# Row sums of a 32 x 512 x 1024 array: each 16-row load issued as two 8-row halves from two engines

## The chip, the cores and the metric

The kernel runs on one core of a Trainium2 chip. The metric is the device time of one execution in microseconds (us). Before the change it is 161.86 us, the median of three runs (161.58 to 162.03).

## The reference

```python
def setup_inputs():
    batch, seq, dim = 32, 512, 1024
    return {"x": np.random.randn(batch, seq, dim).astype(np.float32)}

def reference(x):
    return np.sum(x, axis=-1).astype(np.float32)
```

There are 16,384 rows of 1,024 float32 values, 67.1 MB to be read, and one sum per row to be written, 65.5 KB.

## The kernel before

The rows are cut into 8 groups of 2,048. In a group, each of the 128 partitions holds 16 consecutive rows (`BIG = 16`), which are 64 KB that lie together in HBM. A load of a whole group fills a tile of 128 x 16,384 float32. The tiles come from a pool with three buffers, so a fourth tile has to wait until the first has been read.

The order of the work is written out by hand, with no scheduler. The last group is treated in pieces, so that the kernel starts and ends with something small:

1. The first load (`FIRST = 7`) brings rows 0 to 6 per partition of the last group. It is moved to the program's entry, ahead of the barrier at which the engines meet. VectorE sums its seven rows with one `tensor_reduce` (line 141).
2. Then come the seven other groups, g = 0 to 6, one load of 16 rows each (line 180). Groups 0 to 5 are summed by VectorE, one `tensor_reduce` of 128 x 16,384 each. Of group 6, VectorE sums nine rows one by one with a custom instruction that adds the two halves of a row and accumulates (`halves`, line 155), and ScalarE sums seven with an activation that accumulates (`act`, line 168).
3. At the end come the rest of the last group: a load of six rows, one of two rows, and the last row in two pieces of 560 and 464 values (lines 222 and 223). VectorE and ScalarE share the six and the two rows; VectorE sums the two pieces.
4. Two stores write the sums: ScalarE issues that of the first seven groups (line 191, from line 224), SyncE that of the last group.

All loads are issued by SyncE, in this order. An instruction that issues a DMA waits on its engine's queue, in order, for what it needs: the load of group 1 is held until the seven-row reduction is done (`hold`, line 208), the load of group 2 takes the first buffer again, and each later load waits for the reduction that last read its buffer, that of group 3 for group 0's and so on. The last group's remaining loads use the buffer of group 4.

The functions that the change touches are `rows` (line 177), which issues a load and the sums of its rows, and the loop over the groups that calls it (lines 201 to 208).

Of the kernel before, what the change touches and what calls it, by code (L numbers as in the profile page):

```python
# [100 lines left out]
@with_exitstack  # L101
def kernel(
    ctx: ExitStack,
    tc: tile.TileContext,
    x: bass.AP,
    out: bass.AP,
):
    nc = tc.nc
    nc.at_finalize(issue_first_load_at_entry)
    nc.at_finalize(order_waits)  # L110
    nc.at_finalize(wait_for_the_store_at_the_clear)
    fp32 = mybir.dt.float32
    P = 128
    batch, seq, dim = x.shape
    rows = batch * seq
    J = rows // P
    BIG = 16


    x_g = x.flatten_outer_dims().rearrange("(g p j) d -> g p j d", p=P, j=BIG)  # L120
    out_v = out.rearrange("b s -> (b s)").rearrange("(g p j) -> p g j", p=P, j=BIG)

    def rows_from(j, n):
        return x_g[j // BIG, :, j % BIG : j % BIG + n, :]

    last = J // BIG - 1
    FIRST = 7
    pieces = (560, 464)  # L130

    with (
        tc.tile_pool(name="in", bufs=3) as inpool,
        tc.tile_pool(name="unread", bufs=4, space=bass.MemoryType.PSUM) as upool,
        tc.tile_pool(name="stage", bufs=1) as stpool,
        tc.manual_schedule(),
    ):
        sums = stpool.tile([P, J], fp32)

        def vec(dst, src):  # L140
            return nc.vector.tensor_reduce(  # L141
                out=dst, in_=src, axis=mybir.AxisListType.X, op=mybir.AluOpType.add
            )

        def hold(inst, until, reason):
            tc.add_manual_dep(
                inst.ins,
                until.ins.name,
                mybir.DependencyInfo(mybir.DependencyClass.Sync, mybir.DependencyReason.DATA),
                reason=reason,  # L150
            )

        def halves(dst, src):
            n = src.shape[-1] // 2
            return nc.vector.tensor_tensor_reduce(  # L155
                out=src[:, :n],
                in0=src[:, :n],
                in1=src[:, n:],
                scale=1.0,
                scalar=0.0,  # L160
                op0=mybir.AluOpType.add,
                op1=mybir.AluOpType.add,
                accum_out=dst,
            )

        def act(dst, src, n):
            unread = upool.tile([P, dim], fp32)
            nc.scalar.activation(  # L168
                out=unread[:, :n],
                in_=src,  # L170
                func=mybir.ActivationFunctionType.Copy,
                accum_out=dst,
            )

        sums_of = []

        def rows(t, a, n, j, n_act, pairs=False):
            nv = n - n_act
            block = t[:, a * dim : (a + n) * dim].rearrange("p (n d) -> p n d", d=dim)
            load = nc.sync.dma_start(out=block, in_=rows_from(j, n))  # L180
            if pairs:
                for q in range(nv):
                    sums_of.append(halves(sums[:, j + q : j + q + 1], block[:, q, :]))
            else:
                sums_of.append(vec(sums[:, j : j + nv], block[:, :nv, :]))
            for q in range(nv, n):
                act(sums[:, j + q : j + q + 1], block[:, q, :], dim)
            return load

        def store(eng, g0, g1):  # L190
            return eng.dma_start(
                out=out_v[:, g0:g1],
                in_=sums[:, g0 * BIG : g1 * BIG].rearrange("p (g j) -> p g j", j=BIG),
            )


        j = last * BIG
        t = inpool.tile([P, BIG * dim + 4], fp32)
        rows(t, 0, FIRST, j, 0)
        first = sums_of[-1]  # L200
        for g in range(last):
            t = inpool.tile([P, BIG * dim + 4], fp32)
            if g < last - 1:
                load = rows(t, 0, BIG, g * BIG, 0)
            else:
                rows(t, 0, BIG, g * BIG, 7, pairs=True)
            if g == 1:
                hold(load, first, "no descriptors of later loads while the first ones start")

        t = inpool.tile([P, BIG * dim + 4], fp32)  # L210
        rows(t, FIRST, 6, j + FIRST, 2, pairs=True)
        two = rows(t, FIRST + 6, 2, j + FIRST + 6, 1, pairs=True)
        a = BIG - 1

        j += a
        c, width = pieces
        whole = t[:, a * dim + c : BIG * dim + 2]
        nc.vector.memset(whole[:, width + 1 :], 0.0)  # L220
        part = t[:, a * dim : a * dim + c]
        nc.sync.dma_start(out=part, in_=rows_from(j, 1)[:, 0, :c])  # L222
        nc.sync.dma_start(out=whole[:, 1 : width + 1], in_=rows_from(j, 1)[:, 0, c:])
        hold(store(nc.scalar, 0, last), two, "its packets come behind those of the loads")
        halves(whole[:, :1], part)
        halves(sums[:, j : j + 1], whole)
        store(nc.sync, last, last + 1)
# [30 lines left out]
```

## Time and profile before

| what | value |
|---|---|
| time, median of three runs | 161.86 us (161.58 to 162.03) |
| span of the profiled execution | 159.9 us, no other time is given for that execution |
| VectorE (DVE) busy | 120.6 us, 75% |
| ScalarE (ACT) busy | 12.0 us, 8% |
| read from HBM | 67.11 MB, 420 GB/s over the span |
| a 16-row load, from issue to landing | 40.8 us, median of seven |

A span runs from the first to the last instruction; the time of an execution includes what lies around it. "From issue to landing" includes the time that a load stands behind other loads. A queue (q1, q10) is what one engine issues: q1 is SyncE's and q10 is ScalarE's. The transfers themselves run on 16 DMA engines that the core has. A DMA is cut into packets; here a packet of a load is one partition's share, so that each of the 16 engines moves 8 packets of a load over 128 partitions. In the profile DVE is VectorE, ACT is ScalarE, SP is SyncE, and SPq or ACTq is such an engine's issue of a DMA.

### The profile page before, as it was taken

What the parts mean: (1) busy time and instruction counts of PE and PEld (TensorE: products, weight loads), DVE (VectorE), ACT (ScalarE), POOL (GpSimd) and SP (SyncE); (2) the same over time, 40 slices, a digit from 0 to 9 for tenths busy, and PEclk for the clock granted to TensorE, in tenths of its full rate; (3) what the DMA queues carried; (4) which work ended last, traced back from release to release, by engine and by line L of the source; (5) the groups of instructions that cost most, each with busy time, mean ns of one, the idle gap of its engine ahead of it and who ended that gap; (6) DMA issues with size and microseconds to landing.
All of it is one profiled execution on the core that took longest, in us unless ns stands there. A gap on an engine that the chain in (4) does not pass through costs nothing.

```text
span 159.9 us, 132 instructions
## 1 busy us (share of the span) xinstructions
DVE 120.6 (75%) x40; ACT 12.0 (8%) x21; POOL 0.2 (0%) x4
## 2 busy tenths in 40 slices
DVE  0029600499985999779995899949999499994955
ACT  3000000000000000000000000000000000003993
POOL 0000000000000000000000000000000000000000
DMA  8899899799699699699699699799898996996994
GB/s 308 380 492 525 361 426 525 328 459 525 295 492 525 262 525 525 262 525 525 262 525 508 279 525 476 312 525 410 377 525 361 426 525 262 525 525 289 400 384 124
DMA packets 2784, 67.18 MB, mean 420 GB/s; under 512 B 1248, under 2 KB 1376, under 8 KB 1504
## 3 DMA queue, kind: packets, MB, share of 16 engines
q1 hardware_dynamic: 1872, 67.12, 97.7%
q10 hardware_dynamic: 912, 0.06, 0.4%
HBM read 67.11 MB, written 0.07 MB: 420 GB/s over the span
## 4 chain that ended last, share of the span: by engine, by line
DMA 71%; DVE 27%; SPq 1%; issue 0%; DVEq 0%
DMA t<-in_x_dram 71%; DVE sums L141 26%; SPq L180 0%; SPq L222 0%; DVE t L155 0%; DVEq L253 0%
## 5 line engine op out<-in xcount | busy, mean ns | idle before, releaser
L141 DVE TENSOR_REDUCE sums<-t 128x16 f32<-128x16384 f32 (+1 forms) x7 | 110.9, 15848 | 33.4 <-DMA t<-in_x_dram 33.4
L168 ACT ACTIVATE unread<-t 128x1024 f32<-128x1024 f32 x10 | 10.1, 1013 | 144.7 <-DMA t<-in_x_dram 144.7
L155 DVE CUSTOM_DVE_ANT_0 t<-t 128x512 f32<-128x512 f32 (+2 forms) x16 | 9.6, 654 | 4.1 <-DMA t<-in_x_dram 4.0
L168 ACT ACTIVATION_READ_ACCUMULATOR unread<-t 128x1 f32 x10 | 1.9, 188 | 0.0
L168 ACT ACT_TABLE_LOAD x1 | 1.3, 1283 | 0.8 <-PEq L242 0.8
L155 DVE DVE_READ_ACCUMULATOR2_ANT sums<- 128x1 f32 x15 | 1.2, 81 | 0.0
L242 POOL MEMSET const-bfloat16-1.0<- 128x1 bf16 x1 | 0.1, 102 | 0.0
L242 POOL MEMSET const-uint8-127<- 128x1 uint8 x1 | 0.1, 102 | 0.0
L242 POOL MEMSET const-float32-1.0<- 128x1 f32 x1 | 0.1, 99 | 0.0
L242 POOL MEMSET const-float32-0.0<- 128x1 f32 x1 | 0.1, 98 | 0.2 <-issue 0.2
L155 DVE DVE_READ_ACCUMULATOR2_ANT t<- 128x1 f32 x1 | 0.1, 83 | 0.0
L220 DVE MEMSET t<- 128x1 f32 x1 | 0.1, 59 | 0.0
## 6 DMA issues: line engine op xcount, KB each, us to landing
t<-in_x_dram SPq DMA_DIRECT2D x1, 3584.0 KB, 11.0
t<-in_x_dram SPq DMA_DIRECT2D x1, 3072.0 KB, 28.9
t<-in_x_dram SPq DMA_DIRECT2D x1, 1024.0 KB, 31.0
t<-in_x_dram SPq DMA_DIRECT2D x1, 280.0 KB, 31.2
t<-in_x_dram SPq DMA_DIRECT2D x1, 232.0 KB, 31.3
t<-in_x_dram SPq DMA_DIRECT2D x7, 40.8
out_dram<-sums ACTq DMA_DIRECT2D x1, 56.0 KB, 2.1
out_dram<-sums SPq DMA_DIRECT2D x1, 8.0 KB, 1.4
```

The costliest lines, as they stand in the source:

```text
L141: return nc.vector.tensor_reduce(out=dst, in_=src, axis=mybir.AxisListType.X, op=mybir.AluOpType.add)
L155: return nc.vector.tensor_tensor_reduce(out=src[:, :n], in0=src[:, :n], in1=src[:, n:], scale=1.0, scalar=0.0, op0=mybir.AluOpType.add, op ...
L168: nc.scalar.activation(out=unread[:, :n], in_=src, func=mybir.ActivationFunctionType.Copy, accum_out=dst,)
L220: nc.vector.memset(whole[:, width + 1 :], 0.0)
L242: nc = _bacc.Bacc("TRN2", target_bir_lowering=False, num_devices=1)
```

## The change

A load of 16 rows per partition is issued as two loads of 8 rows, the first half by SyncE and the second by ScalarE, both into the same tile. The other loads (seven, six, two rows and the two pieces) stay as they are. The hold on group 1's load is put on both halves.

```diff
         def rows(t, a, n, j, n_act, pairs=False):
             nv = n - n_act
             block = t[:, a * dim : (a + n) * dim].rearrange("p (n d) -> p n d", d=dim)
-            load = nc.sync.dma_start(out=block, in_=rows_from(j, n))
+            if n == BIG:
+                h = n // 2
+                load = [
+                    nc.sync.dma_start(out=block[:, :h, :], in_=rows_from(j, h)),
+                    nc.scalar.dma_start(out=block[:, h:, :], in_=rows_from(j + h, h)),
+                ]
+            else:
+                load = nc.sync.dma_start(out=block, in_=rows_from(j, n))
...
             if g == 1:
-                hold(load, first, "no descriptors of later loads while the first ones start")
+                for half in load:
+                    hold(half, first, "no descriptors of later loads while the first ones start")
```

In the compiled program ScalarE's queue begins with seven loads of 128 x 8,192, ahead of its table load and its activations. Each `tensor_reduce` waits for both halves of its load. In group 6, VectorE's first eight rows wait for SyncE's half alone; its ninth row and ScalarE's seven rows wait for ScalarE's half.

## The prediction

> **What bounds the kernel now.** I read the engine shares and the DMA queues on the page first.
>
> ```profile
> span 159.9 us, 132 instructions
> ...
> DVE 120.6 (75%) x40; ACT 12.0 (8%) x21; POOL 0.2 (0%) x4
> ...
> q1 hardware_dynamic: 1872, 67.12, 97.7%
> q10 hardware_dynamic: 912, 0.06, 0.4%
> ```
>
> q1 holds everything that SyncE issues, q10 what ScalarE issues. The 16 DMA engines are at work for 97.7% of the span on q1, VectorE for 75%. The chain of waits says the same from the end:
>
> ```profile
> 0.00 11.01 DMA t<-in_x_dram
> ...
> 126.33 31.29 DMA t<-in_x_dram
> 157.62 0.07 issue
> 157.69 0.40 DVE t L155
> ```
>
> The last load lands at 157.62 and one 0.40 us reduction and the store follow. The timeline shows what lies between (start, length, engine; in brackets the idle time before it and who ended it):
>
> ```profile
> 11.03 7.62 DVE L141 TENSOR_REDUCE sums<-t 128x7 f32<-128x7168 f32 x1 [11.03 <-DMA t<-in_x_dram]
> 30.34 17.22 DVE L141 TENSOR_REDUCE sums<-t 128x16 f32<-128x16384 f32 x1 [11.69 <-DMA t<-in_x_dram]
> 49.69 17.22 DVE L141 TENSOR_REDUCE sums<-t 128x16 f32<-128x16384 f32 x1 [2.14 <-DMA t<-in_x_dram]
> ...
> 127.09 17.22 DVE L141 TENSOR_REDUCE sums<-t 128x16 f32<-128x16384 f32 x1 [2.13 <-DMA t<-in_x_dram]
> ...
> 146.50 0.69 DVE L155 CUSTOM_DVE_ANT_0 t<-t 128x512 f32<-128x512 f32 x1 [2.19 <-DMA t<-in_x_dram]
> ...
> 153.87 0.69 DVE L155 CUSTOM_DVE_ANT_0 t<-t 128x512 f32<-128x512 f32 x1 [1.78 <-DMA t<-in_x_dram]
> ```
>
> VectorE waits about 2.1 us for each 16-row load, and they land 19.35 us apart: 8.39 MB each, 433.5 GB/s. The trace's packet records (start and length of every packet) show why. Each of the 16 engines moves 8 packets of 65,536 B per load, 2.418 us long, and the next starts 2.414 us after the one before. The engines are back to back until the last load; no gap in the middle is there to be won. Only less work or a faster packet could shorten the path.
>
> The span is 2.0 us below the median, 161.86. The page gives no other time for the profiled execution, so I carry those 2.0 us over unchanged.
>
> **Part 1: more packets.** A load's 8 packets per engine of 65,536 B become 16 of 32,768 B. The spacing of packets in the records is 2.414 us at 65,536 B, 1.058 us at 28,672 B and 0.908 us at 24,576 B: a line with 0.0368 ns per byte and 3.3 ns per packet. A 32,768 B packet then takes 1.209 us. Seven loads with 8 more packets each cost 56 x 3.3 ns = 0.18 us. Each load ends with a 4-byte packet per engine that counts it done; the next data packet starts 6 ns later. Seven more of these: 0.04 us. All of it is on the path: **+0.22 us**.
>
> That 6 ns row also stands against a rule: the Trainium skill, DMA: Bandwidth & Descriptors, section "Anatomy of one DMA — SWDGE (gpsimd) path", fits about 2.0 us fixed per DMA for those that GpSimd issues. By it, seven more DMAs paid one after the other would cost 14 us. Here the queue's next load starts behind the count packet, so the trace does not charge this.
>
> **Part 2: turns between two rings.** SyncE's and ScalarE's packets now meet on the same engines. The trace of before never shows that: ScalarE's only transfer begins after the loads' last packet. The cost of a turn is bounded below by a gain, the 3.3 ns of each packet hidden behind the other ring (-0.2 us at most for 56 added packets), and above by the longest stretch that a packet in mid-stream shows: some 24,576 B packets near 149 us take about 1.03 us for 0.912, 0.12 us more. With 16 packets per load and engine, at most 112 turns in all, that far end is +13 us. Nearest is the 6 ns row, which is one load giving way to the next on an engine; it is counted already. I take zero for the turn itself.
>
> **Part 3: the issues.** ScalarE issues seven loads ahead of its table load. Before, its queue looked like this:
>
> ```profile
> 0.78 1.28 ACT L168 ACT_TABLE_LOAD   x1 [0.78 <-PEq L242]
> ...
> 146.50 1.03 ACT L168 ACTIVATE unread<-t 128x1024 f32<-128x1024 f32 x1 [144.44 <-DMA t<-in_x_dram]
> ```
>
> The compiled order puts the table load behind the seventh issue, which waits for the reduction of the fourth 16-row load (88.40 + 17.22 = 105.6 us, about 108 below). Its 1.28 us is over by 110, and the first activation is due at 146: 36 us of cover; without it, 1.28 us would come ahead of the ten activations. SyncE's issue count is unchanged (0.33 to 0.44 us each, hidden).
>
> **Part 4: the first load gets company.** ScalarE's first half-load waits for nothing. It leaves at about 0.78 us, where the table load stood, and its packets come some 1.0 us later (the first load's packet starts at 1.02 us, that of ScalarE's store 0.95 us after its issue), so at about 1.8 us, during the first load's first packet. With turns in equal measure, 7 of its packets go between the first load's 8: landing at 11.01 + 7 x 1.21 = 19.5 instead of 11.0, the seven-row reduction ends at 27.1 instead of 18.65, and the hold on the second 16-row load is released then, for both issuers. Packets follow at 28.1. The engines have work until 30.0 (30.34 less 0.36 from last packet to VectorE's start), as the bytes up to there are the same. The cover shrinks from 10.3 us (30.0 - 18.7 - 1.0) to 1.9. Were all 8 packets served first, it would be 20.7, 28.3, 29.3: 0.7 us of cover. So no gap: nothing on the path.
>
> **Part 5: a load is done when its later half is.** At 28.1 SyncE's ring still has (30.0 - 28.1) / 1.21 = 1.6 packets of the first 16-row load, ScalarE's none: up to two packets of the next load slip in, and that load completes up to 2 x 1.21 = **2.4 us later**, at 32.8. ScalarE's ring stays two packets ahead, so each following load completes 2.4 us later too. Only in the last one does it run dry, and SyncE's half finishes where all bytes finish: 146.5 + 0.2. What is late is VectorE: its last long reduction ends at 144.31 + 2.4 + 0.2 = 146.9 instead of 144.31, its nine row sums take 5.6 us (146.50 to 152.10) and end at 152.5. The six-row load lands at 153.87 + 0.2. Its cover was 2.19 + 1.78 = **3.97 us**, 1.5 stay. If it is used up, the excess goes to the end almost one for one, as VectorE's idle time after 153.87 is under 0.2 us. Late buffers hurt nothing: group 3's load is issued at 50.0 while the rings hold work until 69; the tail's loads at 127.6, with work until 146.5.
>
> The sum: 0.22 + 0 = +0.2 us, span 160.1, time **162.1 us**. A measurement can tell about 0.3%, 0.49 us, from no change: this forecast lies within.
>
> A page states the sharing itself: the Trainium skill, DMA: Bandwidth & Descriptors, section "Queues, rings and completion order", has each engine go round the rings packet by packet. No run here shows it; by it part 4 holds as written, with strict order by ring it would be the third rival. The forecast needs less: any lead of one half up to 3.97 us gives the same time.
>
> **Rivals.**
> 1. *VectorE comes late.* If ScalarE's packets begin two to four rounds later (at 3.7 to 6 us, a slow first issue), four of them precede the first load's end, it lands at 15.9, the release is early (24.5 with packets), and the lead is four packets, 4.8 us. That is 0.9 over the cover: 162.1 + 0.9 = 163.0. For it: nothing shows ScalarE's first issue. Against: the table load was up at 0.78.
> 2. *Turns cost* — the rival that is surely slower. At each of about 112 turns an engine loses what its smallest packet takes in all, 7 to 12 ns (64 B, 4 B rows): +0.8 to +1.3 us, 162.9 to 163.4. It decides from 2.4 ns a turn (0.27 us more). At the far end of part 2, 175. For it: alternate packets read other rows of HBM. Against: between different DMAs 6 ns suffice.
> 3. *One ring is served first*, SyncE's say. Then ScalarE's half of the first 16-row load waits for three of SyncE's, lands near 49.7, and VectorE runs back to back: six reductions (103.3 us) to 153, nine rows to 158.6, and what took from 153.87 to 158.09 to 162.8: +4.7, 166.6 us. For it: no row. Against: nothing gives one issuer precedence.
> 4. *Faster.* The first load's first packets take 1.3 to 1.9 us instead of 1.06; ScalarE's could fill up to 0.7 us of that, 161.4. Against: the excess may be HBM's, and more packets are then slow as well.
> 5. *It does not split anything in time*: the halves follow each other. Time as forecast; the compiled order shows the seven issues on ScalarE, so I fold this in.
>
> **Numbers.** Forecast 0.56; VectorE late 0.14 (0.08 of it beyond 0.3%); turns cost 0.16, far end 0.04; one ring first 0.04; faster 0.06. Slower: 0.08 + 0.16 + 0.04 + 0.04 = 0.32. Same: 0.56 + 0.06 = 0.62. Faster 0.06. The range, 161.6 to 163.6, takes in the forecast with the 0.2 us spread of the runs, rival 1 and the near end of rival 2; about 0.18 stays out.
>
> **What would show it.** Part 1: packets of about 1.209 us when alone, q1 and q10 at half each of most bytes, share of both together near 98%. Part 4: the seven-row reduction starts near 19.5. Part 5: 16-row reductions start about 2.4 later than before but 19.4 apart, VectorE's wait ahead of the row sums is gone, the activations start near 144 since ScalarE's half lands early. Rival 2: landings more than 19.5 apart. Rival 1: no wait before the six-row load's sums. I am wrong if the landings drift apart, or if an engine stands empty near 30 us.

## The result and the profile after

The changed kernel takes **162.71 us** (median of four runs, 162.70 to 162.75) against 161.84 us; the ratio is 1.0064 with a 95% interval of 1.0052 to 1.0076. That is slower by some 0.9 us, beyond the 0.3% that a measurement can tell from no change. The forecast was 162.1 us, too near the old time to be told from it. The time lies in the stated range (161.6 to 163.6), but the likeliest case did not come, and the step that failed has to be found.

The engine shares and queues of the changed kernel's page (busy time, share of the span, number of instructions; then each queue's packets, MB and share of the 16 engines' time):

```profile
span 160.6 us, 149 instructions
...
DVE 120.6 (75%) x40; ACT 11.9 (7%) x21; POOL 0.2 (0%) x4
...
q1 hardware_dynamic: 1872, 37.76, 55.2%
q10 hardware_dynamic: 1920, 29.42, 42.9%
```

Both queues together fill 98.1% of the span, as before (97.7 and 0.4): the engines move the same bytes in more time. VectorE's work is the same to 0.1 us. The two issuers, ScalarE's table load and the long waits of VectorE in the changed kernel's timeline:

```profile
0.76 105.99 ACTq L184 DMA_DIRECT2D t<-in_x_dram  x7
0.77 105.95 SPq L183 DMA_DIRECT2D t<-in_x_dram  x7
18.46 7.62 DVE L141 TENSOR_REDUCE sums<-t 128x7 f32<-128x7168 f32 x1 [18.46 <-DMA t<-in_x_dram]
30.70 17.22 DVE L141 TENSOR_REDUCE sums<-t 128x16 f32<-128x16384 f32 x1 [4.61 <-DMA t<-in_x_dram]
50.22 17.22 DVE L141 TENSOR_REDUCE sums<-t 128x16 f32<-128x16384 f32 x1 [2.30 <-DMA t<-in_x_dram]
...
106.79 1.28 ACT L168 ACT_TABLE_LOAD   x1 [106.79 <-DVE sums L141]
...
127.93 17.22 DVE L141 TENSOR_REDUCE sums<-t 128x16 f32<-128x16384 f32 x1 [2.22 <-DMA t<-in_x_dram]
...
147.18 0.69 DVE L155 CUSTOM_DVE_ANT_0 t<-t 128x512 f32<-128x512 f32 x1 [2.03 <-DMA t<-in_x_dram]
147.35 1.03 ACT L168 ACTIVATE unread<-t 128x1024 f32<-128x1024 f32 x1 [39.28 <-DMA t<-in_x_dram]
...
154.50 0.69 DVE L155 CUSTOM_DVE_ANT_0 t<-t 128x512 f32<-128x512 f32 x1 [1.72 <-DMA t<-in_x_dram]
```

The first reduction starts at 18.46 instead of 11.03, so the first load did share its engines. But group 0's starts at 30.70, only 0.36 late, not 2.4. Then the lateness grows slowly: 0.53 at 50.22, 0.84 at 127.93, 0.63 at 154.50. From group 1 on VectorE still waits about 2 us for each load; it is never the one that is late. The end of the chain of waits:

```profile
126.59 31.15 DMA t<-in_x_dram
157.74 0.02 issue
157.77 0.47 DVE t L155 x2
...
158.37 0.40 DVE t L155
```

The end is set by loads as before, 0.68 us later (158.37 against 157.69).

A second thing is not in these rows. The time of a run less its span was 2.15 to 2.21 us in the four runs of the changed kernel (spans are given to 0.1 us). In the 62 runs of the kernel before that stood beside the experiments, it was 1.73 to 1.83, and the mean 1.79. So **about 0.4 of the 0.9 us lies outside the span**, where the prediction had carried 2.0 us over unchanged. (These 2.0 were the median of some runs less the span of one profiled execution.)

The theory after this look (A): the cost has nothing to do with two rings; it is the price of more packets, and something outside the span. The rival (B): packets cost what was predicted, and the second ring the rest.

### The profile page after: what moved, and what is told of

The parts are those of the page before. It is cut to its first block, busy times and chain, and to the rows that moved or that the text cites. A ratio compares the mean times of both kernels' runs of the same rounds, so it can differ in the third digit from the quotient of the medians.

```text
span 160.6 us, 149 instructions
## 1 busy us (share of the span) xinstructions
DVE 120.6 (75%) x40; ACT 11.9 (7%) x21; POOL 0.2 (0%) x4
## 4 chain that ended last, share of the span: by engine, by line
DMA 71%; DVE 27%; SPq 0%; issue 0%; DVEq 0%
DMA t<-in_x_dram 71%; DVE sums L141 26%; DVE t L155 1%; SPq L187 0%; DVEq L155 0%; DVEq L261 0%
## 5 line engine op out<-in xcount | busy, mean ns | idle before, releaser
L168 ACT ACT_TABLE_LOAD x1 | 1.3, 1283 | 106.8 <-DVE sums L141 106.8
```

The source lines that it names most:

```text
L168: nc.scalar.activation(out=unread[:, :n], in_=src, func=mybir.ActivationFunctionType.Copy, accum_out=dst,)
```

## The experiments

Each expectation was written before its kernel ran. Times are medians; a ratio is to the runs of the kernel before on the same chip.

**1. Both halves on SyncE** (`e1_one_ring`).

```diff
-                    nc.scalar.dma_start(out=block[:, h:, :], in_=rows_from(j + h, h)),
+                    nc.sync.dma_start(out=block[:, h:, :], in_=rows_from(j + h, h)),
```

> Both halves of each 16-row load are issued by SyncE: the changed kernel's packets and DMA count on one ring. Theory A (all of the +0.87 us is the price of more packets and more DMAs, whoever issues them): 162.7 us. Theory B (packets and DMAs cost about 0.3 us: 16 x 1.2093 us + 2 x 6 ns against 8 x 2.414 us + 6 ns per load, seven times; the rest, about 0.5 us, comes of the second ring, at the start and in the alternation): 162.1 to 162.2 us, 32,768 B packets 1.209 us apart, first reduction at 11.0 us.

Measured: 162.55 us, ratio 1.0058 (1.0045 to 1.0072), time less span 2.15 to 2.21. Its queues, and the first reductions of its timeline:

```profile
q1 hardware_dynamic: 2880, 67.12, 97.8%
q10 hardware_dynamic: 912, 0.06, 0.3%
```

```profile
10.97 7.62 DVE L141 TENSOR_REDUCE sums<-t 128x7 f32<-128x7168 f32 x1 [10.97 <-DMA t<-in_x_dram]
30.44 17.22 DVE L141 TENSOR_REDUCE sums<-t 128x16 f32<-128x16384 f32 x1 [11.85 <-DMA t<-in_x_dram]
49.87 17.22 DVE L141 TENSOR_REDUCE sums<-t 128x16 f32<-128x16384 f32 x1 [2.21 <-DMA t<-in_x_dram]
69.30 17.22 DVE L141 TENSOR_REDUCE sums<-t 128x16 f32<-128x16384 f32 x1 [2.21 <-DMA t<-in_x_dram]
```

All loads are back on q1, the first load has no company (10.97), and the ratio is the changed kernel's (1.0058 against 1.0064). B falls: the second ring is not the cost.

**2. The changed kernel and the kernel before once more, on one chip** (`after_again`, `before_again`), both as they were.

> The changed kernel beside its variants' chip and the kernel before's. Theory A as it stands now: +0.40 us outside the span; inside it, +0.30 for packets and count packets (seven times 16 x 1.2093 + 0.012 - 8 x 2.414 - 0.006), about +0.15 for packets in mid-stream that take 3 to 5 ns longer from about the 40th on each engine, and +0.15 for the first load's company: about 162.6, 0.1 to 0.2 above the variant with both halves on SyncE. If the second ring cost nothing at all, 162.5.

> The kernel before, for its packet records beside the others'. If mid-stream packets lengthen after a number of packets, whatever their size, its 65,536 B packets keep 2.414 us spacing to about 100 us and lengthen by some ns after; if that first profile's hiccup near 149 us (24,576 B packets of 1.03 us) belonged to that execution alone, it is gone here. Time 161.6, time less span 1.78.

Measured: 162.64 us, ratio 1.0060 (1.0048 to 1.0073), the same as with one ring; and 161.59 for the kernel before, time less span 1.74 to 1.82. The packet records of the two, last count packet of each load in us from the span's start:

| load | before | after | later by |
|---|---|---|---|
| group 0 | 29.98 | 30.05 | 0.07 |
| group 1 | 49.33 | 49.41 | 0.08 |
| group 2 | 68.66 | 68.83 | 0.17 |
| group 3 | 88.00 | 88.27 | 0.27 |
| group 4 | 107.33 | 107.70 | 0.37 |
| group 5 | 126.66 | 127.12 | 0.46 |
| group 6 | 146.00 | 146.57 | 0.57 |
| last piece | 157.10 | 157.69 | 0.59 |

Two slopes: 0.01 us for group 1, then 0.1 a load. The records show what changes in between. Until about 50 us the 32,768 B packets of an engine start 1.2096 us apart on average, and from then on 1.2136, on every engine. In the profiles with 8,192 B packets (below) this begins near 18.5 us. In both it is between the 35th and the 45th packet of an engine. In the kernel before, with half the packets, it comes later: the spacing at 65,536 B is 2.4154 until 50 us, 2.4146 from there to 100 us, and 2.4172 from 100 to 146 us, where an engine has moved 45 packets and more. The hiccup near 149 us of the first profile was indeed that execution's.

**3. Four times the packets, on two rings and on one** (`e3_two_rings_8k`, `e4_one_ring_8k`); the second differs from the first by `nc.sync` in the last line. The 16 sums of a partition and group land in another order than the reference has them; reads and sums are the same in number.

```diff
+                x4 = rows_from(j, n).rearrange("p (a b r) d -> p a b (r d)", a=4, b=2)
+                t4 = block.rearrange("p (b a r) d -> p b a (r d)", a=4, b=2)
                 load = [
-                    nc.sync.dma_start(out=block[:, :h, :], in_=rows_from(j, h)),
-                    nc.scalar.dma_start(out=block[:, h:, :], in_=rows_from(j + h, h)),
+                    nc.sync.dma_start(out=t4[:, 0, :, :], in_=x4[:, :, 0, :]),
+                    nc.scalar.dma_start(out=t4[:, 1, :, :], in_=x4[:, :, 1, :]),
```

> As the change, but each half takes two rows of every four, so that a packet is 8,192 B instead of 32,768 (each group's 16 sums per partition land in another order; the reads and the sums are the same in number). 64 packets per load and engine, 306 ns apart on one ring in the kernel before: 64 x 0.306 + 0.012 = 19.60 us a load against 19.32, +1.9 to 2.0 us. Theory A: 163.8 to 164.4 us, the same as with one ring. Theory B, if each turn between rings costs 3 ns beyond that: 448 turns, 1.3 us more, and the start's part: 165.2 us.

> As the kernel with 8,192 B packets on two rings, but SyncE issues both halves (each group's 16 sums per partition land in another order). Theory A: the same as that kernel. Theory B: +1.96 us for packets and DMAs alone, 163.8 us.

Measured: 165.85 us on two rings, 165.81 on one, ratios 1.0261 (1.0247 to 1.0275) and 1.0259 (1.0245 to 1.0273). 448 turns more or less cost nothing: B is dead here too. But both are 1.4 to 2 us above theory A's 163.8 to 164.4. The page of the one-ring kernel:

```profile
span 163.7 us, 145 instructions
...
q1 hardware_dynamic: 8256, 67.12, 98.6%
```

The queue is full as ever, so packets cost more than the line had said. Its span is 3.85 us above that of the kernel before (163.65 against 159.8). At the spacing of the first 18 us, 0.306 us, packets would make 7 x (64 x 0.306 + 0.012 - 19.330) = 1.9 of that (19.330 is 8 x 2.4155 + 0.006, a whole load). The records show the rest: over all seven loads the spacing is 0.3101 on average, and 448 x 0.0041 = 1.8. Sum 3.7.

**4. Group 0 whole** (`e2_group0_whole`): the first load without company, two rings from group 1 on.

```diff
-            if n == BIG:
+            if n == BIG and j > 0:
```

> Group 0's load stays whole on SyncE, groups 1 to 6 are split as in the change: the first load has no company. Theory A: 6/7 of the cost stays, 162.6 us. Theory B: the start's part goes (0.14 us by the mean landing of group 0, 29.88 against 29.71 us, less 0.03 for its packets) with 0.04 of packets, 162.5 us. Theory C (the whole rest of 0.5 us is the start's): 162.1 us. The first reduction starts near 11.0 us again in all three.

Measured: 162.96 us, ratio 1.0088 (1.0073 to 1.0103): every theory missed, it is slower than with all seven split. Its timeline on VectorE, with ScalarE's issues:

```profile
11.04 7.62 DVE L141 TENSOR_REDUCE sums<-t 128x7 f32<-128x7168 f32 x1 [11.04 <-DMA t<-in_x_dram]
18.69 92.94 ACTq L184 DMA_DIRECT2D t<-in_x_dram  x6
35.21 17.22 DVE L141 TENSOR_REDUCE sums<-t 128x16 f32<-128x16384 f32 x1 [16.55 <-DMA t<-in_x_dram]
...
132.88 17.22 DVE L141 TENSOR_REDUCE sums<-t 128x16 f32<-128x16384 f32 x1 [2.20 <-DMA t<-in_x_dram]
...
150.01 0.68 DVE L155 CUSTOM_DVE_ANT_0 t<-t 128x512 f32<-128x512 f32 x1
150.62 0.08 DVE L155 DVE_READ_ACCUMULATOR2_ANT sums<- 128x1 f32 x1
```

This is the prediction's first rival, in the flesh. The hold opens at 18.69 and ScalarE's packets begin at 22.23, when SyncE's ring has three of group 0's 65,536 B packets left on each engine. Four packets of 1.21 us go ahead of its end: 30.34 + 4.84 = 35.2, and 35.21 is what stands there. The lead lasts; the row sums start at 150.01 without a wait (no bracket) instead of 146.50, and the cover of 3.97 us is used up. The last reduction ends 1.1 us behind that of the one-ring variant (159.59 against 158.52) in the profiled executions, 0.5 by the median spans (160.9 and 160.4); the profiled execution here was the slowest of four (163.41 us), with longer packets between 50 and 100 us.

This trace holds something against a simple count of packets. Its 32,768 B packets are 1.2094 us apart until 50 us and 1.2103 between 100 and 146 us, though each engine has moved 74 packets by 100 us: the lengthening to 1.2136 is not there.

**5. What lies outside the span.** Six more DMAs that move nothing to speak of (`e5_tiny6`), and 14 more instructions on GpSimd (`e7_memset14`):

```diff
+            if g == 0:
+                tiny = stpool.tile([P, 16 * 6], fp32)
+                for k in range(6):
+                    nc.sync.dma_start(out=tiny[:1, 16 * k : 16 * k + 16], in_=rows_from(k, 1)[:1, 0, :16])
```

```diff
+        spare = stpool.tile([P, 14], fp32)
+        for k in range(14):
+            nc.gpsimd.memset(spare[:, k : k + 1], 0.0)
```

> The kernel before, with six loads of 64 B more (one partition each, nobody reads them), issued by SyncE right behind group 0's load. The time less the span was 1.78 us in every run of the kernel before and 2.13 to 2.21 in runs with seven more DMAs. Theory D (each DMA of a program costs some 0.05 us outside the span, however small): time less span 2.05 to 2.15 us, span at most 0.1 us longer (six packets on one engine), time about 162.0 where the kernel before has 161.58. Theory E (what lies outside comes of large loads or of waits for two halves): 1.78 us, time 161.6 to 161.7.

> The kernel before, with 14 memsets of one column more on GpSimd, which has nothing else to do. If the time outside the span grows with the number of instructions of any kind, time less span goes from 1.78 to 2.1 us or more; if it is DMAs alone, it stays at 1.78 and the time at 161.6.

Measured: 161.57 and 161.68 us, ratios 0.9995 (0.9985 to 1.0006) and 0.9998 (0.9988 to 1.0008), time less span 1.78 and 1.80 on average. Neither DMAs nor instructions at large: D falls.

Then VectorE's second wait (`f1_two_waits`), the same split with no second wait (`f2_halves_summed`), and three split loads instead of seven (`f3_three_split`). The first adds to the six 64 B loads, kept in a list:

```diff
+            if g < last - 1:
+                hold(sums_of[-1], tinies[g], "a second semaphore to wait for")
```

the other two change the one-ring variant:

```diff
+                if n == BIG:
+                    vec(sums[:, j : j + h], block[:, :h, :])
+                    sums_of.append(vec(sums[:, j + h : j + nv], block[:, h:nv, :]))
```

```diff
-            if n == BIG:
+            if n == BIG and j < 3 * BIG:
```

> The kernel before, whole loads, with the six 64 B loads again; now each long reduction of groups 0 to 5 also waits for one of them, which has landed long ago. So VectorE waits for two DMAs before each, as in the changed kernel, and nothing else is different from the run with six 64 B loads (time less span 1.78, time as before). Theory F (0.4 us outside the span comes of VectorE's waits for two loads): time less span 2.1 to 2.2, time 0.3 to 0.5 above the kernel before. Theory G (it comes of the split loads themselves): 1.78 and no change.

> As the variant with both halves on SyncE, but VectorE sums each half by a reduction of its own as it lands (groups 0 to 5), so that none of them waits for two loads. Theory F: time less span back to 1.8, time 162.1 to 162.2. Theory G: 2.18 as in that variant, 162.5. The six half reductions that come late in each load are hidden either way.

> As the variant with both halves on SyncE, but only groups 0, 1 and 2 are split; 3 to 6 stay whole. If every part of the cost goes by the number of split loads, 3/7 of +0.95: +0.4 us, time less span 1.95. If mid-stream packets lengthen only where small packets follow the 40th on an engine (from about 50 us on), that part is nearly gone: +0.13 for packets plus what lies outside the span.

Measured:

| kernel | time, ratio (95%) | time less span, mean | VectorE's instructions in the trace |
|---|---|---|---|
| two waits | 161.98, 1.0017 (1.0007 to 1.0028) | 2.16 | 55 |
| halves summed | 162.55, 1.0047 (1.0029 to 1.0064) | 2.20 | 55 |
| three split | 161.87, 1.0004 (0.9995 to 1.0014) | 1.78 | 52 |

Two waits alone, with whole loads and a span of 159.8 (median), give 2.16; that speaks for F. Split loads without the second wait give 2.20 all the same; that speaks against it. Both theories fall. What the kernels with 2.2 us have in common is the length of VectorE's program, its semaphore instructions included (a second wait is one): 55, against 49 in the kernel before and those with tiny loads or GpSimd's memsets, 52 with three split loads, and 54 in experiment 4, where it was 2.01 to 2.07.

A last run makes the program longer and nothing else (`f4_memset12`):

```diff
+        spare = stpool.tile([P, 12], fp32)
+        for k in range(12):
+            nc.vector.memset(spare[:, k : k + 1], 0.0)
```

> The kernel before, with 12 memsets of one column more on VectorE at the very start, where it waits until 11 us anyway: no load, no wait is changed. VectorE's instruction records are 49 in the kernel before, 52 with three loads split, 54 with six, 55 with seven; the time less the span was 1.78, 1.78, 2.05 and 2.16 to 2.20 us. Here there are 61. Theory H (what lies outside the span goes by the length of VectorE's program, in one step near 54): 2.18 us, time about 0.4 above the kernel before. Theory H2 (a slope beyond 53, 0.13 us an instruction): 2.9 us. Theory I (it comes of split loads or waits for two semaphores after all): 1.78 us and no change.

Measured: 162.39 us, ratio 1.0047 (1.0031 to 1.0064), time less span 2.15 to 2.21 with 61 instructions. Its memsets in the timeline (start, length; the bracket is the idle time before them):

```profile
0.85 0.37 DVE L141 MEMSET spare<- 128x1 f32 x12 [0.85 <-PEq L245]
10.95 7.62 DVE L144 TENSOR_REDUCE sums<-t 128x7 f32<-128x7168 f32 x1 [9.72 <-DMA t<-in_x_dram]
```

They are over 9.72 us before the first load lands, so they delay no reduction, and the 0.4 us outside is there. H2 and I fall, and theory H holds: the time less span rises between 52 and 55 instructions, from 1.8 to 2.2 us with 2.05 at 54, and six more add nothing. What takes those 0.4 us stays open: from the store's issue to the end of the span the traces show the same 1.7 to 1.8 us in both kernels. Behind the span, the records of this run alone have a packet of 8,192 B of the kind "instruction" (161.95 us); the other kernels with 2.2 us have none there, so it settles nothing. The span of this kernel was 160.2, 0.4 above its neighbours; its packets between 90 and 140 us lengthened by some 0.5 us in the profiled execution. The kernel before has spans of 159.7 to 160.5 from run to run; whether the 0.4 is such a spread or the memsets' doing, no run here shows.

## Why the prediction was right or wrong

**The sum, against the same chip's kernel before (+0.93 us in experiment 2, medians 162.64 and 161.71):** about 0.4 outside the span, and 0.6 inside it by the profiles of that experiment (0.59 at the last packet; the two profiled executions are 162.61 and 161.57, 1.04 apart). Of these 0.59, packets at their early spacing make 7 x (16 x 1.2096 + 0.012 - 19.330) = 0.25, and the later spacing of 1.2136 in five loads 5 x 16 x 0.0040 = 0.32. The first load's company and the tail share what is left, 0.02.

- **What bounds the kernel: right.** The engines stay full, and no experiment came out faster than the kernel before.
- **"I carry those 2.0 us over unchanged": wrong**, the largest miss, 0.4 us. The second wait of six reductions took VectorE's program from 49 to 55 instructions, over the rise. A kernel with whole loads pays nearly the same (2.16).
- **Part 1: right in kind, mis-sized.** 0.22 predicted, and 0.25 at the early spacing. But from about the 40th packet of an engine on, the packets are 4 ns further apart, another 0.32. The step that failed is the line through three sizes, which gave a packet one price for the whole run; at 3.3 ns a packet, 4 ns more is double. Why they lengthen isn't shown. That two rings are not the cause is shown by experiments 1 and 3. That it goes by the number of packets is only argued, from where it begins, and experiment 4, where the same packets on two rings did not lengthen, speaks against the number alone. (In `f3_three_split`, 65,536 B packets follow 48 split ones an engine, and are 2.418 us apart instead of 2.4155.)
- **Part 2: right.** A turn between rings costs nothing (162.55 against 162.64, 165.81 against 165.85). In the records of one engine the packets alternate strictly, one of each ring, 1.209 us apart. This is what the Trainium skill, DMA: Bandwidth & Descriptors, section "Queues, rings and completion order", says of packets; the section "Issuing engines are not separate DMA queues", that a second issuer saves only issue time, agrees with 1.0060 against 1.0058.
- **Part 3: right.** The table load came at 106.8, 40 us before its first use.
- **Part 4: right that no gap opens, wrong on the start.** ScalarE issued at 0.76, but its first packets began at 4.70, not 1.8: 3.9 us after the issue, where a store whose packets find the engines free needs 0.95. Five or six of its packets then went between those of the first load, which let the first reduction start at 18.46 (19.5 predicted). The cover at 30 us was enough.
- **Part 5: wrong, and without cost.** The same delay at the release (issue at 26.11, first packet at 30.89) let SyncE's ring finish group 0 first. So no lead arose: from group 1 on both halves of a group end within 0.01 us of each other, group 0 was 0.36 late instead of 2.4, and the activations started at 147.35, not near 144.
- **Rivals.** *VectorE late*: ScalarE's packets did begin in the stretch that was named (4.70), but the price was not paid, since the lead needs a prompt release as well. Experiment 4 shows the mechanism and its cover real, at 0.5 to 1.1 us where 0.9 was named. *Turns cost*: the time came out just under its low end (162.9) for another reason. *One ring first*, *faster*: nothing of either.

The chance for slower was 0.32; the two terms that made it so, the step outside the span and the lengthened packets, were in no case of the prediction. That the time lies in the range is luck in this sense: the range reached up to 163.6 for rivals 1 and 2, and neither of them is what was paid.

## What to carry to other kernels

Where the DMA engines are back to back, a second issuer has nothing to give, and halving the size of the packets is paid on the path: count packets per engine, and look for their price in the records late in the run too, not only in a few early ones. A load that is split gives its reader two semaphores to wait for, whoever issues the halves; here such a wait was one more instruction, and a longer program can cost time that no row of the span shows, so time less span should be compared run by run. When two issuers share engines, look at who is ahead when a hold opens: a lead of four packets stayed for the whole run in experiment 4, and whether it costs anything is decided by the idle time of the last reader.

## What was not expected of the hardware

- Time less span went from 1.8 to 2.2 us between 52 and 55 instructions on VectorE, whatever they were: second waits, reductions, memsets. At 61 it was still 2.2.
- A ring that starts while another keeps the engines busy showed its first packet 3.5 to 5.2 us after the issue (0.76 to 4.70, 18.69 to 22.23, 26.11 to 30.89, and 0.79 to 5.96 with 8,192 B packets); where the engines were free it was 0.84 to 1.02 us.
- From around the 40th packet on each engine, packets are about 3 to 5 ns further apart in the kernels with split loads, but for that of experiment 4: 0.306 to 0.310 us at 8,192 B, 1.2096 to 1.2136 at 32,768 B.
